# Searches in alternating pairs, and the background of an activation phase as three paced streams

## The chip, the cores and the metric

One core of a Trainium2 chip runs the whole kernel. Its engines are TensorE (PE; its weight loads are shown apart as PEld), VectorE (DVE), ScalarE (ACT), GpSimd (POOL) and SyncE (SP, which here only issues transfers). The metric is the device time of one execution in microseconds, lower is better; the figure of a kernel is the median of its runs.

## The reference

One layer of a streaming encoder over 512 tokens of width 1024. First a token mixer (a gated short convolution and a gated linear recurrence), which this change does not touch. Then a channel part that looks up experts by product keys, which is where all of this takes place. Cut to its core:

```
N_KEYS, PEER_HEADS, PEER_TOPK = 128, 8, 16          # 128*128 experts
q  = (xb @ w_q).reshape(p, PEER_HEADS, 2, 64)
sc = einsum('phcd,hcnd->phcn', q, sub_keys)          # scores of 128 sub-keys, twice per head
top_s, top_i = top_k(sc, 16)                         # stage 1: 16 of 128, for c = 0, 1
cand_s = top_s[:, :, 0, :, None] + top_s[:, :, 1, None, :]
cand_i = top_i[:, :, 0, :, None] * N_KEYS + top_i[:, :, 1, None, :]
best_s, best_pos = top_k(cand_s, 16)                 # stage 2: 16 of the sums
idx = take_along_axis(cand_i, best_pos)
g   = softmax(best_s)
act  = gelu(einsum('phkd,pd->phk', expert_u[idx], xb))
out  = einsum('phk,phkd->pd', g * act, expert_v[idx])
```

The layer ends with a gated residual add and a final RMSNorm.

## The kernel before

The 512 tokens stand in four tiles of 128 (`t` = 0 to 3). Tokens from 192 on (320 of them, `NU`) are treated densely: the activations of all 16,384 experts are computed by TensorE, 128 experts at a time, and multiplied by a gate that is zero for experts not chosen. The first 192 tokens are treated sparsely for the activation: the chosen rows of `expert_u` are gathered from HBM by GpSimd's indirect transfers, and a dot product on VectorE (`scr`) gives each activation. Tile 0 is sparse to the end: for it rows of `expert_v` are gathered and summed (`ys`). The 64 tokens of tile 1 in between (`XB`) have sparse activations and dense outputs.

All large products are made of three matmuls in a rounded format: weights are loaded as `wraw`, ACT rounds them to `whi`, DVE subtracts to get the remainder `wlo`, and each block is multiplied high by high, high by low and low by high (lines 90, 91, 92). DVE's `wlo` of a chunk is thus needed before TensorE reaches the chunk's third matmul.

The stages that matter here, in order of time:

- **Query phase** (to about 310 us): queries and sub-key scores; the 32 stage 1 searches of heads 0 to 3 are woven in by the scheduler.
- **Activation phase** (from about 310 us; `CE` = 124 of the 128 "u" chunks before the next phase begins): a chunk is 24 matmuls into `ps_act` and a gelu on ACT (`act`). Beside this runs the background work: the remaining stage 1 searches, the four `topk_tile`, the gates, and the dots.
- **Output phase** (from about 878 us): 128 "v" chunks of 18 matmuls into `acc`, together with the last four "u" chunks; the dots that are left and the 128 row sums of tile 0 run beside it.

A search (`top16`, lines 448 to 454) is five operations of VectorE: the eight largest, their places, the same values struck out, the next eight, their places. Each reads what the operation before wrote. Stage 1 searches 128 scores (`top`, `sc`), stage 2 searches 64 candidate sums (`best`, `cand`).

A gate group (`gates_step`) serves four tokens: DVE compares for one factor (`jh`, line 601) and part of the other (`igh`, line 611), ACT makes the rest of `igh` by two activations (lines 608 and 609), TensorE multiplies them (`ps_gt`, line 617), ACT copies the result to a staging tile (`stg`, line 626), and every four groups SP stores it to HBM (`Gd`); one of these stores, the last, is issued by ACT. There are 96 groups: 80 for tiles 1 (second half), 2 and 3, which need only the top-k of their tile, and 16 for the `XB` tokens, which need their 64 dots first. The output phase loads gates back (`gt`, line 858) and multiplies them with `act` (`cf`, line 880).

The order in the activation phase is fixed when the kernel is built: in that part nothing is rescheduled, and every engine runs its instructions in the order in which they were written. A planner keeps an estimate of time for PE, DVE and ACT (`pe`, `dve`, `ac`). After each chunk it takes steps from generators as long as DVE's estimate is behind PE's; each step `yield`s what it costs on DVE, or `None` for "not before the next chunk". In the kernel before there are two generators, the background `bg` and the dots `dot_gen`. The background is one long sequence: searches, top-k of tile 1, the remaining searches, top-k of tile 0, gates of tile 1 mixed with the top-k of tile 2, gates of tile 2 mixed with the top-k of tile 3, gates of tile 3, gates of the `XB` tokens. `SH` sets the share of the dots. In the loop of chunk `k`, DVE's work for the chunk after next (`wlo` of `k + 2`) is written first, and the background steps follow it.

Of the kernel before, what the change touches and what calls it, by code (L numbers as in the profile page):

```python
# [8 lines left out]
F32 = mybir.dt.float32  # L9
# [11 lines left out]
NT = 4  # L21
NE = 128
# [12 lines left out]
def block_kernel(ctx, tc, xT, small, w_ada1, w_ada, b_ada, w_in, w_r, w_i, w_out, w_q, keys, uT, u, v, final_g, out):  # L35
    nc = tc.nc
# [196 lines left out]
    z_, tn, e_, w_, w2, ac = (l4[:, i, :] for i in range(6))  # L233
# [85 lines left out]
    for cb in range(4):  # L319
# [14 lines left out]
        r = mt("r")  # L334
# [3 lines left out]
        s = mt("s")  # L338
# [4 lines left out]
        a = mt("a")  # L343
# [5 lines left out]
        h = mt("h")  # L349
# [92 lines left out]
    scp = ep.enter_context(tc.tile_pool(name="scp", bufs=1, side="right"))  # L442
# [2 lines left out]
    scx = ExitStack()  # L445
    scs = scx.enter_context(tc.tile_pool(name="scs", bufs=1, side="right"))

    def top16(best, where, s, width):
        rep = scp.tile([128, 128], F32, name="rep", bufs=2)[:, :width]
        nc.vector.max(out=best[:, 0:8], in_=s)  # L450
        nc.vector.max_index(out=where[:, 0:8], in_max=best[:, 0:8], in_values=s)
        nc.vector.match_replace(out=rep, in_to_replace=best[:, 0:8], in_values=s, imm_value=-3.0e38)
        nc.vector.max(out=best[:, 8:16], in_=rep)
        nc.vector.max_index(out=where[:, 8:16], in_max=best[:, 8:16], in_values=rep)

    sc = {}

    def stage1(heads, tiles):
        for t in tiles:
            for h in heads:  # L460
                for c in range(2):
                    top16(top[:, t, h, c], ti[:, t, h, c], sc[h, c][:, t, :], 128)
                    yield 1000

    qsp = {}
    early = chain(*(stage1([h], range(NT)) for h in range(HQ)))
# [52 lines left out]
    selT = {}  # L519
# [4 lines left out]
    def topk_tile(t):  # L524
# [11 lines left out]
        yield 1900  # L536
        best = topk.tile([128, 8, 16], F32, name="best")
        pos = topk.tile([128, 8, 16], U32, name="pos")
        for h in range(8):
            top16(best[:, h], pos[:, h], cand[:, h, :], 64)  # L540
            yield 700
        g = g_s.rearrange("p (h k) -> p h k", h=8) if t == 0 else topk.tile([128, 8, 16], F32, name="g")
        nc.vector.tensor_sub(g, best, best[:, :, 0:1].to_broadcast([128, 8, 16]))
        msk = topk.tile([128, 8, 16], U32, name="msk")
# [35 lines left out]
        else:  # L580
# [9 lines left out]
            if t == 1:  # L590
# [4 lines left out]
                for e in range(2):  # L595
                    nc.vector.tensor_copy(idx_b[XB * e:XB * (e + 1), :], idf[0:XB, XB * e:XB * (e + 1)])
        yield 1200

    def gates_prep(sl, t0, aoh):
        jh = topk.tile([128, 4, 128], F32, name="jh", bufs=3)  # L600
# [19 lines left out]
    gst = {}  # L620
# [37 lines left out]

    stgp = []

    def merge(a, b, share):
        da = db = 0.0
        live = [a, b]
        while live:
            g = a if (len(live) == 2 and da * (1 - share) <= db * share) or live == [a] else b
            if g not in live:
                g = live[0]
            n = next(g, 0)
            if n == 0:
                live.remove(g)  # L670
                continue
            if g is a:
                da += n or 1200
            else:
                db += n or 1200
            yield n
# [67 lines left out]
    def dots():  # L744
        for n, (_, hn, dst, k) in enumerate(usteps):
            for m in range(n, min(n + ahead() - 1, len(usteps))):
                assert m < XB or len(sready) == 2
                gath(u, usteps[m][0], usteps[m][3], m)
            scr = rowp.tile([128, D], F16, name="scr")
            nc.vector.scalar_tensor_tensor(scr, rows.pop(n), 1.0, hn, op0=OP.mult, op1=OP.mult,  # L750
                                           accum_out=dst[:, k:k + 1])
# [5 lines left out]
            yield 1270  # L757

    def sums():
        for k in range(128):  # L760
            for kk in range(k, min(k + ahead() - 1, 128)):
                gath(v, idx_s, kk, kk)
            if k == 0:
                nc.vector.tensor_scalar(ys, rows.pop(k), acts[:, 0:1], None, op0=OP.mult)
            else:
                nc.vector.scalar_tensor_tensor(ys, rows.pop(k), acts[:, k:k + 1], ys, op0=OP.mult, op1=OP.add)  # L766
            if k == 3:
                coef_gelu(1)
            if k == 8:
                coef_gate(1)  # L770
            yield 1270


    hd = lambda k: h2h[:, k, T - NU:]
# [108 lines left out]
            nc.scalar.activation(ch, cf, AF.Copy)  # L883
            coef[n + 2] = (cf, ch)

    bg = background_E()
    dot_gen = dots()
    pe, dve, ac = [0], [0], [0]
    td = tb = 0
    first = None  # L890
    done = False
    for k in range(5):
        w_load(k)
    for k in range(3):
# [5 lines left out]
    for k in range(CE):  # L900
        weights(k)
        u_chunk(k, psE)
        if sready and first is None:
            first = k + 4
# [3 lines left out]
        dve[0] = max(dve[0], RHO * pe[0] - LEAD)  # L908
        hold = done
        xd = 0  # L910
        while dve[0] < RHO * pe[0] or (k == CE - XE - 1 and not done):
            if done and xd >= XD:
                break
            if first is not None and k >= first and (hold or td * (1 - SH) < tb * SH or (gst and ac[0] > pe[0] + AD)):
                n = next(dot_gen, None)
                if n:
                    dve[0] += n
                    td += n
                    xd += 1
                    continue  # L920
            if hold:
                break
            n = next(bg, 0)
            if n == 0:
                done = hold = True
                kb = k
                continue
            if n is None:
                hold = k < CE - XE - 1
                continue  # L930
            dve[0] += n
            if first is not None:
                tb += n
        w_high(k + 3)
        if k == CE - XE - 1:
# [44 lines left out]
        nc.vector.tensor_add(frow[0], frow[0], frow[1])  # L980

    sparse = chain(dot_gen, sum_gen)
    steps, given = len(usteps) - len(bdone) + 128, 0
    for k in range(CE, len(jobs)):
        w_load(k + 5)
        w_high(k + 3)
        w_low(k + 2)
        kind, n = jobs[k]
        if kind == "u":
            u_chunk(k, psP)  # L990
        else:
            v_gates(n + 5)
            v_coef(n)
            vsp[n] = [w.pop(k).rearrange("p k e -> p (k e)") for w in (whi, wlo)] + list(coef.pop(n))
            if n < NE - VT:
                for b in range(3):
                    v_chunk(n, b)
                del vsp[n]
            u_evict()
            pe[0] += 4090  # L1000
            dve[0] += 2005
        if kind == "v":
            share = min((n + 1) / (NE - VE), 1) * (steps + 0.31 * (NE - RB)) - 0.31 * max(n + 1 - RB, 0)
            while given < share and next(sparse, None):
                given += 1
    fin = vp.tile([128, 2, 3, D], F32, name="gt", bufs=1)
    final_rows()
    manual.close()
# [42 lines left out]
LEAD = 3500  # L1051
RHO = 1.0
VE = 1
SH = 0.44
XD = 1
CE = 124
GB_E = 4
# [55 lines left out]
```

## Time and profile before

| what | us |
|---|---|
| median of 3 runs | 1439.85 (1435.31 to 1441.27) |
| the profiled execution's own time | 1442.91 |
| its span, first to last instruction | 1441.1 |
| TensorE busy | 1368.3 |
| VectorE busy | 1258.8 |
| ScalarE busy | 750.2 |
| GpSimd busy | 488.7 |

The profiled execution is 3.06 us above the median, and 1.8 us of its time lies outside the span. TensorE's matmuls overlap, so that a matmul whose duration is given as 0.31 us may start every 0.147 us; a short rest of the engine does not always show as idle time, and starts are the better measure. The same is true of VectorE: the next operation may start before the end shown for the one before. A row of the waits reads: engine, tile and line that waited; what ended the wait; total, number and longest wait in us. The mark q behind an engine means its queue, which issues transfers.

### The profile page before, as it was taken

To read this page: it belongs to the slowest core of one execution; us is meant where nothing else is said; L and a number is where in the kernel's file an instruction comes from. 1 tells how busy PE (TensorE), PEld (TensorE's weight loads), DVE (VectorE), ACT (ScalarE), POOL (GpSimd) and SP (SyncE) were. 2 spreads that over 40 slices of the span, in tenths; PEclk is the share of its full clock that TensorE was granted. 3 is DMA by queue.
4 is the path that set the end of the run, shared out by engine and by line. 5 is a ranking of instruction groups with operands and counts; after the bars stand their busy time and mean duration, and the time that the engine had idled before them with its cause. 6 is when DMAs were issued, how large, how long until landed. Compare 5 with 4: busy or idle time off the path is not lost.

```text
span 1441.1 us, 22491 instructions
## 1 busy us (share of the span) xinstructions
PE 1368.3 (95%) x7739; PEld 1179.2 (82%) x7739; DVE 1258.8 (87%) x2600; ACT 750.2 (52%) x1336; POOL 488.7 (34%) x334
## 2 busy tenths in 40 slices
PE   6999998999988998989999997999999999999995
PEld 2566787789988988989999997877788888888884
DVE  6776555898999999989999995889989899999998
ACT  3554433435433678889999543433434344343443
POOL 0000000000232343234344343556655565655550
PEclk9999999999999999999999998999999999999998
DMA  9575322124588989989999999999999999999994
GB/s 382 201 273 188 120 86 91 66 97 147 188 282 273 317 281 321 335 297 319 349 379 368 354 366 363 342 384 408 405 410 404 411 404 412 411 412 411 410 376 174
DMA packets 160759, 440.14 MB, mean 305 GB/s; under 512 B 16258, under 2 KB 68482, under 8 KB 158596
## 3 DMA queue, kind: packets, MB, share of 16 engines
q1 hardware_dynamic: 113636, 267.76, 50.6%
q0 software_dynamic: 46720, 169.89, 31.1%
q8 instruction: 61, 1.00, 0.3%
q10 hardware_dynamic: 288, 1.05, 0.2%
q14 instruction: 54, 0.44, 0.1%
HBM read 393.54 MB, written 45.09 MB: 304 GB/s over the span
## 4 chain that ended last, share of the span: by engine, by line
PE 44%; DVE 20%; issue 16%; DMA 13%; POOL 3%; ACT 3%; SPq 0%; DVEq 0%; ACTq 0%; POOLq 0%
PE acc L967 17%; DMA wraw<-in_v_dram 7%; PE ps_z L90 5%; PE ps_z L92 5%; PE ps_z L91 5%; DVE scr L750 4%; DVE wlo L81 4%; POOL rows L730 3%; DMA rows<-in_u_dram,idx_s 2%; PE ps_act L90 2%; PE ps_act L91 2%; PE ps_act L92 2%; DMA rows<-in_u_dram,idx_b 2%; DVE cl L873 1%; PE ps_gt L617 1%
## 5 line engine op out<-in xcount | busy, mean ns | idle before, releaser
L76 ACT ACTIVATE whi<-wraw 128x1024 fp32r<-128x1024 f32 x292 | 308.2, 1056 | 315.3 <-DMA wraw<-in_v_dram 127.6
L81 DVE TENSOR_TENSOR wlo<-wraw,whi 128x1024 fp32r<-128x1024 f32 x292 | 355.8, 1219 | 72.8 <-ACT whi L76 71.6
L92 PE MATMUL ps_act<-h,wlo 128*128 128x320 f32 x1024 | 319.3, 312 | 9.9 <-DVE wlo L81 9.7
L90 PE MATMUL ps_act<-h,whi 128*128 128x320 f32 x1024 | 323.1, 316 | 3.5 <-ACT act L816 2.3
L91 PE MATMUL ps_act<-h,whi 128*128 128x320 f32 x1024 | 317.9, 310 | 0.0
L730 POOL DMA_INDIRECT rows<-in_u_dram,idx_s x128 | 192.7, 1506 | 226.5 <-DVE scr L750 208.5
L730 POOL DMA_INDIRECT rows<-in_v_dram,idx_s x128 | 197.8, 1545 | 150.2 <-DVE ys L766 123.6
L967 PE MATMUL acc<-whi,ch 128*128 128x512 f32 x750 | 233.1, 392 | 9.2 <-ACT act L816 7.4
L967 PE MATMUL acc<-whi,cl 128*128 128x512 f32 x750 | 233.5, 393 | 0.4
L967 PE MATMUL acc<-wlo,ch 128*128 128x512 f32 x750 | 232.0, 390 | 0.0
L92 PEld LDWEIGHTS ps_act<-h,wlo 128*128 128x128 f32 x1024 | 193.5, 189 | 13.9 <-DVE wlo L81 13.9
L90 PEld LDWEIGHTS ps_act<-h,whi 128*128 128x128 f32 x1024 | 194.0, 189 | 4.4 <-ACT act L816 2.9
L91 PEld LDWEIGHTS ps_act<-h,whi 128*128 128x128 f32 x1024 | 193.8, 189 | 0.2
L730 POOL DMA_INDIRECT rows<-in_u_dram,idx_b x64 | 93.0, 1453 | 254.5 <-DVE scr L750 109.8
L967 PEld LDWEIGHTS acc<-whi,ch 128*128 128x128 f32 x750 | 141.1, 189 | 40.3 <-ACT act L816 8.2
L967 PEld LDWEIGHTS acc<-whi,cl 128*128 128x128 f32 x750 | 140.1, 188 | 34.1 <-DVE cl L873 5.7
L967 PEld LDWEIGHTS acc<-wlo,ch 128*128 128x128 f32 x750 | 141.4, 189 | 29.8
L766 DVE SCALAR_TENSOR_TENSOR ys<-rows,acts,ys 128x1024 f32<-128x1024 f32 x127 | 162.6, 1280 | 1.5
L750 DVE SCALAR_TENSOR_TENSOR scr<-rows,h2n 128x1024 f16<-128x1024 f32 x128 | 156.1, 1219 | 6.0 <-DMA rows<-in_u_dram,idx_s 4.4
L883 ACT ACTIVATE ch<-cf 128x384 fp32r<-128x384 f32 x128 | 67.3, 526 | 120.1 <-DVE cf L880 116.7
L617 PE MATMUL ps_gt<-igh,jh 128*128 128x128 f32 x768 | 99.7, 279 | 13.7 <-DVE jh L601 8.0
L816 ACT ACTIVATE act<-ps_act 128x320 f32<-128x320 f32 x128 | 55.2, 432 | 107.0 <-PE ps_act L92 106.7
(258 smaller groups left out, 1879.7 us busy)
## 6 DMA issues: line engine op xcount, KB each, us to landing
wraw<-in_uT_dram SPq DMA_DIRECT2D x128, 512.0 KB, 5.4
wraw<-in_v_dram SPq DMA_DIRECT2D x128, 512.0 KB, 9.6
Gd<-stg SPq DMA_DIRECT2D x46, 512.0 KB, 7.2
wada<-in_w_ada_dram SPq DMA_DIRECT2D x16, 1024.0 KB, 5.1
Ad<-act SPq DMA_DIRECT2D x96, 160.0 KB, 6.9
act<-Ad SPq DMA_DIRECT2D x96, 160.0 KB, 10.7
h<-Gd SPq DMA_DIRECT2D x12, 1024.0 KB, 15.3
wraw<-in_w_in_dram SPq DMA_DIRECT2D x20, 512.0 KB, 5.8
```

The source lines that it names most:

```text
L76: nc.scalar.activation(hi, raw, AF.Copy)
L81: nc.vector.tensor_sub(lo, raw, hi.bitcast(F32))
L90: nc.tensor.matmul(ps, hi[:, k, :], xh(k), start=first and k == ks[0], stop=False)
L91: nc.tensor.matmul(ps, hi[:, k, :], xl(k), start=False, stop=False)
L92: nc.tensor.matmul(ps, lo[:, k, :], xh(k), start=False, stop=last and k == ks[-1])
L617: nc.tensor.matmul(pg[:, :, k], jh[:, k, :], ig[:, k, :], start=True, stop=True)
L730: nc.gpsimd.indirect_dma_start(out=r[:, :], out_offset=None, in_=table, in_offset=bass.IndirectOffsetOnAxis(ap=idxs[:, k:k + 1], axis=0))
L750: nc.vector.scalar_tensor_tensor(scr, rows.pop(n), 1.0, hn, op0=OP.mult, op1=OP.mult, accum_out=dst[:, k:k + 1])
L766: nc.vector.scalar_tensor_tensor(ys, rows.pop(k), acts[:, k:k + 1], ys, op0=OP.mult, op1=OP.add)
L816: nc.scalar.activation(act[c], ps, AF.Gelu)
L883: nc.scalar.activation(ch, cf, AF.Copy)
L967: nc.tensor.matmul(accs[b][e], st[:, bs], mv[:, e * 512:(e + 1) * 512], start=first, stop=last)
```

## The change

1. `top16` takes two searches at once and writes each of the five operations for the one and then for the other. Its planned cost goes from 1000 ns to 2 x 1150 for a pair of stage 1, and from 700 to 2 x 850 for one of stage 2.
2. The background is cut into three generators beside the dots: `searches_E` (top-k of tiles 1, 2, 0, 3), `rest_E` (the stage 1 searches of tiles 2, 0, 3), and `gates_E` (all gates, each tile from the chunk after its top-k). The function `turn` picks one after each chunk: gates when fewer have been given than a straight line from the first possible chunk (`gopen`) to `KG` = 4 chunks before the end asks for, searches by a budget per chunk (`NS`), the remaining searches against a number of dots per chunk (`DS`), and the dots otherwise.
3. The top-k of tile 0, on which the dots of tile 0 wait, now comes third instead of second. A dot costs 1320 in the plan instead of 1270, and DVE is planned to run up to 6000 ns further ahead in the first nine chunks (`HEAD`).

The diff, cut:

```diff
-    def top16(best, where, s, width):
-        rep = scp.tile([128, 128], F32, name="rep", bufs=2)[:, :width]
-        nc.vector.max(out=best[:, 0:8], in_=s)
...
+    def top16(two, width, cost):
+        reps = [scp.tile([128, 128], F32, name="rep", bufs=2)[:, :width] for _ in two]
+        for best, where, s in two:
+            nc.vector.max(out=best[:, 0:8], in_=s)
+        for best, where, s in two:
+            nc.vector.max_index(out=where[:, 0:8], in_max=best[:, 0:8], in_values=s)
+        for rep, (best, where, s) in zip(reps, two):
+            nc.vector.match_replace(out=rep, in_to_replace=best[:, 0:8], in_values=s, imm_value=-3.0e38)
+        yield 1.2 * cost
+        for rep, (best, where, s) in zip(reps, two):
+            nc.vector.max(out=best[:, 8:16], in_=rep)
+        for rep, (best, where, s) in zip(reps, two):
+            nc.vector.max_index(out=where[:, 8:16], in_max=best[:, 8:16], in_values=rep)
+        yield 0.8 * cost
...
-        for h in range(8):
-            top16(best[:, h], pos[:, h], cand[:, h, :], 64)
-            yield 700
+        for h in range(0, 8, 2):
+            yield from top16([(best[:, j], pos[:, j], cand[:, j, :]) for j in (h, h + 1)], 64, 850)
...
-    def background_E():
+    def searches_E():
         heads = range(HQ, 8)
         yield from stage1(heads, [1])
         yield from topk_tile(1)
         sready.append(1)
-        yield from stage1(heads, [0, 2, 3])
+        while not gopen:
+            yield None
+        yield from topk_tile(2)
+        yield from topk_tile(0)
+        sready.append(0)
+        yield from topk_tile(3)
+
+    def rest_E():
+        yield from stage1(range(HQ, 8), [2, 0, 3])
         scx.close()
         stgp.append(ep.enter_context(tc.tile_pool(name="stgp", bufs=1, side="right")))
-        yield from topk_tile(0)
-        sready.append(0)
-        yield from merge(gates_tile(1, range(4, 8), selT[1]), topk_tile(2), 0.32)
-        yield from merge(gates_tile(2, range(8), selT[2]), topk_tile(3), 0.48)
-        yield from gates_tile(3, range(8), selT[3])
+        gopen.append(cur[0])
+
+    def gates_E():
+        for t in range(1, NT):
+            while gready.get(t, NE) > cur[0]:
+                yield None
+            yield from gates_tile(t, range(4 if t == 1 else 0, 8), selT[t])
         while len(bdone) < XB:
-            yield next(dot_gen)
+            yield None
...
+    def turn(k):
+        awake = [g for g in "gsrd" if g in gens and asleep[g] <= k]
+        if gopen and "g" in gens:
+            gt = 96 * (k + 1 - gopen[0]) / (KD - KG - gopen[0])
+            if "g" in awake and given["g"] < gt and ac[0] < pe[0] + AD:
+                return "g"
+            if "s" in awake and (given["g"] < gt and ac[0] < pe[0] + AD or given["s"] < NS * (k - gopen[0]) / (KD - gopen[0])):
+                return "s"
+        elif "s" in awake:
+            return "s"
+        elif "r" in awake and ("d" not in awake or given["d"] >= DS * (k - first[0])):
+            return "r"
+        for g in "dsg" if ac[0] < pe[0] + AD else "ds":
+            if g in awake:
+                return g
...
-            if first is not None and k >= first and (hold or td * (1 - SH) < tb * SH or (gst and ac[0] > pe[0] + AD)):
-                n = next(dot_gen, None)
...
-            n = next(bg, 0)
+            n = next(gens[g], 0)
```

What this does to the order of instructions is seen best at two places. The first is VectorE around the 25th of the 124 chunks, each begun by its `wlo` (line 81). Before, there stand pairs of dots (`scr`), then single searches (`top`, `ti`, `rep`), and no gates:

```order
L81 TENSOR_TENSOR wlo<-wraw,whi 128x1024
L750 SCALAR_TENSOR_TENSOR scr,act_b<-rows,h2b 128x1024 x2
L81 TENSOR_TENSOR wlo<-wraw,whi 128x1024
L450 MAX top<-sc 128x8
L451 MAX_INDEX ti<-top,sc 128x8
L452 MATCH_REPLACE rep<-top,sc 128x128
L453 MAX top<-rep 128x8
L454 MAX_INDEX ti<-top,rep 128x8
L750 SCALAR_TENSOR_TENSOR scr,act_b<-rows,h2b 128x1024
```

After, in the same place, a gate group (`jh`, `igh`) follows each `wlo`, then dots or part of a pair of narrow searches (`best`, `pos`):

```order
L81 TENSOR_TENSOR wlo<-wraw,whi 128x1024
L606 TENSOR_TENSOR jh<-iota,selT 128x512
L616 TENSOR_SCALAR igh<-iota,selT 128x128
L751 SCALAR_TENSOR_TENSOR scr,act_b<-rows,h2b 128x1024 x2
L81 TENSOR_TENSOR wlo<-wraw,whi 128x1024
L606 TENSOR_TENSOR jh<-iota,selT 128x512
L616 TENSOR_SCALAR igh<-iota,selT 128x128
L451 MAX best<-cand 128x8 x2
L453 MAX_INDEX pos<-best,cand 128x8 x2
L455 MATCH_REPLACE rep<-best,cand 128x64 x2
L751 SCALAR_TENSOR_TENSOR scr,act_b<-rows,h2b 128x1024
```

The wide searches of this stretch have moved some chunks ahead, gates have moved here from about chunk 48 on, and the operations of two searches alternate (x2).

The second place is ScalarE from the last copies of gates (`stg`) to the first gate that the output phase reads (`cf`). Before, three copies stand in one chunk, then the last store of gates, and four pairs of `whi` and `act` before the `cf`:

```order
L626 ACTIVATE stg<-ps_gt 128x128x4 x3
L637 DMA Gd_2592<-stg 128x1024 x2
L76 ACTIVATE whi<-wraw 128x1024
L816 ACTIVATE act<-ps_act 128x320
L76 ACTIVATE whi<-wraw 128x1024
L816 ACTIVATE act<-ps_act 128x320
L76 ACTIVATE whi<-wraw 128x1024
L816 ACTIVATE act<-ps_act 128x320
L76 ACTIVATE whi<-wraw 128x1024
L816 ACTIVATE act<-ps_act 128x320
L76 ACTIVATE whi<-wraw 128x1024
L879 ACTIVATE cf<-gt 128x64
```

After, the last copy comes a chunk ahead of the store, and two more pairs of `whi` and `act` (six, the first three shown) stand between the store and the `cf`:

```order
L631 ACTIVATE stg<-ps_gt 128x128x4
L76 ACTIVATE whi<-wraw 128x1024
L817 ACTIVATE act<-ps_act 128x320
L642 DMA Gd_2592<-stg 128x1024 x2
L76 ACTIVATE whi<-wraw 128x1024
L817 ACTIVATE act<-ps_act 128x320
L76 ACTIVATE whi<-wraw 128x1024
L817 ACTIVATE act<-ps_act 128x320
L76 ACTIVATE whi<-wraw 128x1024
L817 ACTIVATE act<-ps_act 128x320
```

The store has moved two chunks ahead; on TensorE the last `ps_gt` has moved from behind the chunk numbered 118 to behind 114.

Over the phase, in the order: 118 dots stand ahead of the `wlo` numbered 128, against 122 before; the gates run in chunks 22 to 36, 46 to 67 and 88 to 113 instead of 46 to 118; and around chunks 70 to 77, until the top-k of tile 0 is done, no dots can be given.

More of the change, by code (lines that the diff above doesn't have):

```diff
@@ L460, in stage1 @@
             for h in heads:
-                for c in range(2):
-                    top16(top[:, t, h, c], ti[:, t, h, c], sc[h, c][:, t, :], 128)
-                    yield 1000
+                yield from top16([(top[:, t, h, c], ti[:, t, h, c], sc[h, c][:, t, :]) for c in range(2)], 128, 1150)
     qsp = {}
@@ L597, in topk_tile @@
         yield 1200
+        gready[t] = cur[0] + 1
     def gates_prep(sl, t0, aoh):
@@ L659, in block_kernel @@
     stgp = []
[L661 to L676, printed above, removed]
     sready = []
-    def background_E():
+    cur, gready, gopen = [0], {}, []
+    def searches_E():
         heads = range(HQ, 8)
@@ L746, in dots @@
             for m in range(n, min(n + ahead() - 1, len(usteps))):
-                assert m < XB or len(sready) == 2
+                while m >= XB and len(sready) < 2:
+                    yield None
                 gath(u, usteps[m][0], usteps[m][3], m)
@@ L756, in dots @@
                 coef_gate(0)
-            yield 1270
+            yield 1320
     def sums():
@@ L884, in v_coef @@
             coef[n + 2] = (cf, ch)
[L886 to L891, printed above, removed]
+    gens = {"s": searches_E(), "r": rest_E(), "g": gates_E(), "d": dots()}
+    dot_gen = gens["d"]
+    pe, dve, ac = [0], [-HEAD], [0]
+    late_k = {}
+    asleep = {"s": 0, "r": 0, "g": 0, "d": NE}
+    given = {"s": 0, "r": 0, "g": 0, "d": 0}
+    KD = CE - XE - 1
+    first = []
+    def turn(k):
[13 more added lines that the diff above has]
+                return g
     for k in range(5):
@@ L902, in block_kernel @@
         u_chunk(k, psE)
-        if sready and first is None:
-            first = k + 4
+        cur[0] = k
+        if sready and not first:
+            first.append(k + 4)
+            asleep["d"] = k + 4
             for m in range(GB_E - 1):
@@ L907, in block_kernel @@
         ac[0] = max(ac[0], pe[0] - LEAD)
-        dve[0] = max(dve[0], RHO * pe[0] - LEAD)
-        hold = done
+        dve[0] = max(dve[0], RHO * pe[0] - LEAD - (HEAD if k < 9 else 0))
         xd = 0
-        while dve[0] < RHO * pe[0] or (k == CE - XE - 1 and not done):
-            if done and xd >= XD:
-                break
-            if first is not None and k >= first and (hold or td * (1 - SH) < tb * SH or (gst and ac[0] > pe[0] + AD)):
-                n = next(dot_gen, None)
[L916 to L922, printed above, removed]
-            n = next(bg, 0)
+        while dve[0] < RHO * pe[0] or k == KD:
+            g = turn(k)
+            if k == KD:
+                g = next((g for g in "sg" if g in gens), None)
+                if "s" not in gens and len(bdone) < XB:
+                    g = "d"
+            if g is None or (g == "d" and "g" not in gens and xd >= XD):
+                break
+            n = next(gens[g], 0)
             if n == 0:
-                done = hold = True
-                kb = k
+                assert g != "d"
+                late_k[g] = k
+                del gens[g]
                 continue
             if n is None:
-                hold = k < CE - XE - 1
+                asleep[g] = k + 1
                 continue
             dve[0] += n
-            if first is not None:
-                tb += n
+            xd += g == "d"
+            if gopen or g == "d":
+                given[g] += 1 if g in "gd" else n
         w_high(k + 3)
-        if k == CE - XE - 1:
+        if k == KD:
             ep.close()
@@ L982, in block_kernel @@
     sparse = chain(dot_gen, sum_gen)
-    steps, given = len(usteps) - len(bdone) + 128, 0
+    steps, done = len(usteps) - len(bdone) + 128, 0
     for k in range(CE, len(jobs)):
@@ L1003, in block_kernel @@
             share = min((n + 1) / (NE - VE), 1) * (steps + 0.31 * (NE - RB)) - 0.31 * max(n + 1 - RB, 0)
-            while given < share and next(sparse, None):
-                given += 1
+            while done < share and next(sparse, None):
+                done += 1
     fin = vp.tile([128, 2, 3, D], F32, name="gt", bufs=1)
@@ L1053 @@
 VE = 1
-SH = 0.44
+KG = 4
+HEAD = 6000
+NS = 60000
+DS = 1.0
 XD = 1
```

6 lines of the change are left out of this document (1 added, 5 removed).

## The prediction

> **What bounds the kernel now.** I read the page's engine shares first, then stretches of time, the matrix engine's waits, and single rows. The stretches of the activation phase (128 chunks of 24 matmuls, 124 of them before the first `acc`) come first; columns are stretch, length, busy us of PE, PEld, DVE, ACT, POOL with instruction counts, granted clock, DMA share, GB/s.
>
> ```profile
> PE 1368.3 (95%) x7739; PEld 1179.2 (82%) x7739; DVE 1258.8 (87%) x2600; ACT 750.2 (52%) x1336; POOL 488.7 (34%) x334
> 309.60:872.40 562.80, 536.04 (x3755) 528.58 (x3755) 521.37 (x1295) 381.58 (x723) 182.45 (x123) 0.99 0.85 301
> 309.60:386.00 76.40, 75.50 (x504) 75.23 (x505) 68.03 (x253) 36.42 (x51) 3.86 (x4) 0.98 0.46 157
> 386.00:471.00 85.00, 75.03 (x486) 71.04 (x485) 80.75 (x255) 33.15 (x44) 29.56 (x20) 1.00 0.78 260
> 471.00:565.00 94.00, 89.34 (x622) 87.92 (x623) 89.59 (x199) 69.95 (x129) 31.97 (x22) 1.00 0.88 307
> 565.00:700.00 135.00, 124.49 (x878) 123.11 (x877) 123.56 (x272) 117.97 (x248) 49.10 (x33) 0.97 0.92 323
> 700.00:800.00 100.00, 100.00 (x756) 100.00 (x755) 96.49 (x190) 94.95 (x208) 42.56 (x28) 1.00 1.00 367
> 872.40:886.40 14.00, 6.57 (x17) 4.67 (x15) 9.34 (x14) 5.71 (x11) 3.86 (x3) 0.63 1.02 343
> 886.40:1150.00 263.60, 261.43 (x1170) 213.80 (x1169) 239.26 (x350) 104.68 (x185) 150.30 (x101) 1.00 1.01 393
> 1150.00:1400.00 250.00, 250.00 (x1105) 207.00 (x1104) 240.20 (x281) 107.59 (x189) 144.68 (x93) 1.00 1.03 407
> ```
>
> PE never rests from 700 to 800 and after 1150, though DVE and ACT are about 95% busy there. It does rest 10.0 us in 386–471, 4.7 in 471–565, 10.5 in 565–700, and at the change of phase 17 matmuls take 14 us. Its waits in 309.6–887:
>
> ```profile
> PE ps_act L92 <- DVE wlo L81: 9.7, 12, 1.4
> PE ps_gt L617 <- DVE jh L601: 8.0, 4, 2.7
> PE acc L967 <- ACT act L816: 7.4, 2, 5.0
> PE ps_gt L617 <- ACT sqd L608: 2.6, 1, 2.6
> ```
>
> Next, PE's own price. Two L90 matmuls, 96 apart (four chunks), and two gate groups in the chain of waits:
>
> ```profile
> 315.57 0.31 PE L90 MATMUL ps_act<-h,whi 128*128 128x320 f32 x1
> 329.65 0.31 PE L90 MATMUL ps_act<-h,whi 128*128 128x320 f32 x1
> 820.50 1.78 PE ps_gt L617 x16
> ```
>
> A chunk is 14.08 / 4 = 3.52 us, a gate group 0.89. So 124 chunks and 96 groups are 436.5 + 85.4, with some 2 us of small transposes 524 us, against 562.8: 39 lost. Of those 39, the clock takes about 1.5 in the first stretch (0.02 of 76) and 3.5 in 565–700 (0.03 of 135 at most); about 30 are stalls, the rest jitter. From 872.4 to 886.4 the 17 matmuls are worth 17 x 0.226 (250 / 1105) = 3.8 us: 10 lost. In all 49 us.
>
> **Searches in pairs.** In the activation phase a search runs alone, each instruction reading what the one before wrote; in the query phase before it the scheduler already wove two searches. Starts of like instructions, alone, woven, then alone on 64 candidates:
>
> ```profile
> 320.37 0.28 DVE L450 MAX8 top<-sc 128x8 f32<-128x128 f32 x1
> 320.68 0.09 DVE L451 MATCH_VALUE_LOAD ti<-top,sc 128x8 f32 x1
> 321.94 0.28 DVE L450 MAX8 top<-sc 128x8 f32<-128x128 f32 x1
> ...
> 271.43 0.28 DVE L450 MAX8 top<-sc 128x8 f32<-128x128 f32 x1
> 271.63 0.27 DVE L453 MAX8 top<-rep 128x8 f32<-128x128 f32 x1
> 272.59 0.28 DVE L450 MAX8 top<-sc 128x8 f32<-128x128 f32 x1
> ...
> 328.37 0.21 DVE L450 MAX8 best<-cand 128x8 f32<-128x64 f32 x1
> 329.60 0.21 DVE L450 MAX8 best<-cand 128x8 f32<-128x64 f32 x1
> ```
>
> Alone 1.57 us, woven 1.16: the next start comes 0.20 behind a MAX8 instead of 0.31 when it does not need its result. The pair is that woven form, so a wide search saves 0.41. For the narrow one (1.23) no woven row exists: between saving 0 and 0.41; I take the same three dependent steps at 0.11, so 0.90. 32 wide and 32 narrow searches of the phase: 13.1 + 10.6 = 24 us less on DVE. The query phase gains nothing, being woven already.
>
> [...]
>
> **The three streams.** Prices of the other DVE work:
>
> ```profile
> 720.46 0.68 DVE L601 TENSOR_TENSOR jh<-iota,selT 128x512 f32<-128x512 f32 x1
> 721.06 0.59 DVE L611 TENSOR_SCALAR igh<-iota,selT 128x128 f32<-128x128 f32 x2
> 721.57 1.21 DVE L750 SCALAR_TENSOR_TENSOR scr<-rows,h2n 128x1024 f16<-128x1024 f32 x1
> ...
> 722.83 1.23 DVE L750 SCALAR_TENSOR_TENSOR scr<-rows,h2n 128x1024 f16<-128x1024 f32 x1
> 723.98 1.22 DVE L81 TENSOR_TENSOR wlo<-wraw,whi 128x1024 fp32r<-128x1024 f32 x1
> 725.12 0.69 DVE L601 TENSOR_TENSOR jh<-iota,selT 128x512 f32<-128x512 f32 x1
> ```
>
> Start to start: `jh` 0.60, `igh` 0.26 each, a dot 1.15 to 1.26 (1.2), `wlo` 1.14. With these, the search prices and the counts of the two orders, DVE against PE in us per stretch, numbered by the `wlo` that the work stands ahead of (small operations at 0.2 to 0.6, the 2048-wide ones at 1.25):
>
> before: 22–39 DVE 74, PE 64; 40–57 71, 68; 58–90 153, 153; 91–107 88, 90; 108–120 61, 62.
> after: 22–39 75, 77; 40–57 76, 82; 58–90 124, 131; 91–107 85, 88; 108–120 58, 59.
>
> The 10 us that DVE is over in 22–39 before are the 10.0 that PE rests in 386–471, so the sum holds. Afterwards PE is the longer one everywhere: gates, which PE does, stand where formerly only DVE worked, and the searches are cheaper. The cover is thin in 91–107 (3 us), but 700–800 shows that density, two gate groups a chunk, running without rest, with ACT at 94.95 of 100; the new order is hardly anywhere denser for ACT. The dots stop around chunks 70–77, as tile 0's top-k comes later, but nothing of this phase waits for them; otherwise they come at 1.2 a chunk as before, so POOL's gathers, each behind the dot that frees its buffer, keep their pace.
>
> What stays: the cold start 1.5, jitter 4, one wait for ACT at the first top-k 1. New: gates now begin, or double their rate, three times (in the loops of chunks 22, 46 and 88), each needing DVE a chunk further ahead; I charge each the mean `jh` wait, 8.0 / 4 = 2.0. One half-clock spell costs 1.7. Sum 14, so 39 − 14 = 25 gained. Bounds: 0 (each removed wait returns as another) and 34 (only start and jitter stay).
>
> [...] Here the clock mean of 0.97 stands in 565–700, where no single wait exceeds 2.7, so I keep the spell.
>
> **The change of phase.** Who waits there: SP's load of the first gates, behind PE's last gates and the last store; DVE then; the store itself:
>
> ```profile
> SPq L858 <- DMA Gd<-stg: 6.5, 1, 6.5
> SPq L858 <- PE ps_gt L617: 2.2, 1, 2.2
> 855.65 0.82 ACTq L637 DMA_DIRECT2D Gd<-stg  x2
> 874.30 0.49 DVE L880 TENSOR_TENSOR cf<-act,gt 128x320 f32<-128x320 f32 x1 [7.42 <-DMA gt<-Gd]
> 875.49 1.06 ACT L76 ACTIVATE whi<-wraw 128x1024 fp32r<-128x1024 f32 x1 [9.47 <-DMA wraw<-in_uT_dram]
> ```
>
> While SP stands 8.7 us, the weight loads queued behind it are late, ACT waits 9.47 for one, and the `act` that frees PSUM stands behind it. In the new order PE's last gate group comes four chunks earlier (14 us) and the store's place on ACT two chunks (7 us), no longer held by `ps_gt`. SP's stop nearly goes; what is late next is the 512 KB gate load itself, which lands close to its use. I leave 4 of the 10: 6 gained (bounds 0 to 10).
>
> **Dots left over.** By the same chunk 118 dots are done instead of 122, so four rows of 128 x 4 KB, 2.1 MB, move into the second phase. At 407 GB/s that is 5.2 us if transfers bind, 0 if they don't; in 1150–1400 PE rests nowhere at 407, in 886–1150 it loses some 4. I take 2.
>
> **Sum.** −25 − 6 + 2 = −29 against the profiled run's own 1442.91 (span 1441.1): 1413.9. That run is 3.06 over the median of 1439.85, so 1411.
>
> **Rivals.** (1) Transfers take it back: the last chunks now run at 3.52 us without gates, while dots, weights and gate loads come as before; the DMA share is 1.02 there already. Then the change of phase keeps its 10 and the dots cost 5.2: −25 + 5 = −20, 1420. (2) Dots or gates hold each other: each of the 27 single gate groups woven with narrow searches (loops 22–36 and 55–66) waits 0.4 more than charged: 11 us, 1422. Against it: DVE's sum is under PE's there. [...] (4) Slower: every one of those 27 groups makes PE wait the 2.0 us of the `jh` row, since gates, searches and dots alternate on DVE with no lead: 54 us, less the 29: 1465; it decides once more than 14 of the 27 wait so. Against it: after its waits of 565–700 PE had none for 100 us at twice the gate density.
>
> **Chances.** As worked out 0.66 (its own range 1400 to 1421); rival 1 0.13, rival 2 0.10, rival 3 0.06, rival 4 0.05. The range reaches from 1400 (stalls all but gone, 34 + 10 − 5 off) to 1431, leaving out rivals 3 and 4 and the luckiest tenth. Faster by over 0.5% (7 us, about what a measurement of this kernel tells from no change) 0.89, within 0.06, slower 0.05.
>
> **What would show it.** Paired searches at 1.16 and 0.90 us; no `wlo` wait of PE in chunks 22–40; under 12 us of PE rest between 310 and the first `acc`; that `acc` near 849; SP's wait at the gate load under 2; the second phase within 3 us of its old length. I am wrong if PE waits for `ps_gt` once per woven gate group, or if the second phase loses pace to transfers.

## The result, and the profile after

The changed kernel takes 1417.0 us (median of 4 runs, 1415.15 to 1418.33) against 1440.56 for the kernel before in the same runs; the ratio is 0.9843, 95% interval 0.9815 to 0.9871. The profiled run took 1418.33 itself (span 1416.6), 24.6 us less than the 1442.91 (span 1441.1) of the one before.

Stretches of the changed kernel, with the columns of the prediction (length, busy us and instructions of PE, PEld, DVE, ACT, POOL, clock, DMA share, GB/s): the activation phase, the change of phase, the output phase to its last `acc`, and four closer looks at the output phase:

```profile
309.40:838.40 529.00, 526.42 (x3754) 524.91 (x3755) 498.98 (x1281) 383.35 (x727) 183.97 (x119) 1.00 0.87 317
838.40:852.00 13.60, 7.30 (x19) 5.23 (x18) 9.03 (x14) 5.72 (x11) 4.19 (x3) 0.62 1.03 347
852.00:1402.60 550.60, 542.15 (x2385) 445.54 (x2384) 511.14 (x679) 223.47 (x394) 303.68 (x198) 0.99 0.99 387
963.50:984.40 20.90, 17.58 (x74) 13.07 (x73) 16.65 (x27) 6.91 (x12) 12.47 (x9) 1.00 1.04 415
984.40:1002.40 18.00, 18.00 (x72) 14.67 (x73) 17.86 (x29) 7.79 (x14) 11.12 (x7) 0.91 0.91 327
1035.10:1056.10 21.00, 18.47 (x74) 14.54 (x73) 17.53 (x28) 8.48 (x15) 10.65 (x7) 0.92 1.04 411
1056.10:1072.40 16.30, 16.30 (x74) 13.50 (x72) 16.23 (x19) 7.08 (x13) 10.47 (x7) 1.00 1.03 415
```

The output phase before, cut in the same place:

```profile
886.40:1426.30 539.90, 537.48 (x2386) 442.06 (x2385) 505.59 (x668) 222.41 (x394) 297.14 (x195) 1.00 1.00 391
```

The same cuts before are 562.8, 14.0, 539.9 (to the last `acc` at 1426.3) and then 14.8 to the end; now 529.0, 13.6, 550.6 and 14.0. So the 24.5 us of span are −33.8, −0.4, +10.7 and −0.8, and 0.2 that the phase begins earlier: the activation phase gained more than the whole change did, and the output phase gave a third of it back. PE's waits from 309.4 to 853, all of them:

```profile
PE acc L987 <- ACT act L817: 6.3, 2, 3.9
PE ps_act L90 <- ACT sc L494: 1.2, 1, 1.2
PE ps_gt L622 <- ACT stg L631: 0.9, 1, 0.9
PE ps_gt L622 <- ACT igh L614: 0.8, 2, 0.5
PE ps_act L90 <- ACT act L817: 0.4, 1, 0.4
PE ps_gt L622 <- DVE igh L616: 0.3, 1, 0.3
```

The waits for `wlo` (9.7) and `jh` (8.0) are gone; the one at the change of phase (first row) is not. The searches, each row now two instructions (the two halves of a narrow pair, and the start of the next pair):

```profile
320.61 0.35 DVE L451 MAX8 best<-cand 128x8 f32<-128x64 f32 x2
321.65 0.35 DVE L458 MAX8 best<-rep 128x8 f32<-128x64 f32 x2
322.31 0.34 DVE L451 MAX8 best<-cand 128x8 f32<-128x64 f32 x2
```

A pair starts 1.70 us behind the one before it: 0.85 a search, against 1.23 alone. At the change of phase, SP's issues of the gate loads and what stood behind them (the second row is the next weight load's issue):

```profile
823.26 7.21 SPq L859 DMA_DIRECT2D gt<-Gd  x3
830.58 3.03 SPq L71 DMA_DIRECT2D wraw<-in_uT_dram  x1
835.64 6.87 SPq L859 DMA_DIRECT2D gt<-Gd  x3
838.09 0.49 DVE L881 TENSOR_TENSOR cf<-act,gt 128x320 f32<-128x320 f32 x1 [5.27 <-DMA gt<-Gd]
840.54 1.06 ACT L76 ACTIVATE whi<-wraw 128x1024 fp32r<-128x1024 f32 x1 [8.34 <-DMA wraw<-in_uT_dram]
```

SP no longer waits for the gates' store, but the issue of three loads itself holds it for 7.21 us; the weight load behind them is 7 us late and ACT waits 8.34 for it. The same loads before, in three closer views of SP (855 to 856.2, 862.3 to 862.95, 870 to 877.55):

```profile
855.02 1.00 SPq L858 DMA_DIRECT2D gt<-Gd  x2
862.55 0.36 SPq L858 DMA_DIRECT2D gt<-Gd  x1
870.09 7.43 SPq L858 DMA_DIRECT2D gt<-Gd  x3
```

The first three were issued in 1.4 us, with the 6.5 us wait for the store between the second and the third; the next three, with no wait among them, took 7.43 already. In the output phase PE waits 2.6 and 2.5 us in two places (at 981 and 1039); what was waited for in the few us around each:

```profile
PE acc L987 <- ACT ch L884: 2.6, 1, 2.6
ACT whi L76 <- DMA wraw<-in_v_dram: 7.4, 1, 7.4
...
PE acc L987 <- ACT ch L884: 2.5, 1, 2.5
DVE cf L881 <- DMA act<-Ad: 4.0, 1, 4.0
```

And the two transfers in the chain of waits of that stretch (start, length):

```profile
964.16 18.31 DMA wraw<-in_v_dram
1020.49 17.95 DMA act<-Ad
```

A weight load took 18.31 us and an activation load 17.95, where their medians in this kernel are 10.0 and 11.0, at DMA shares of 1.03 and 1.04. Each wait is followed by about eight matmuls at half clock, 0.43 us instead of 0.227 (clocks of 0.51 from 984.9 to 988.3 and 0.50 from 1043.1 to 1046.3, which make the 0.91 and 0.92 above). So the two cost some 4.6 us each: 2.6 to 2.8 for the wait and some 1.6 for the spell, the rest in short gaps beside them. The second shows in one stretch, the sixth above: 72 matmuls take 21.0 us, 16.3 in the quiet seventh. The first wait lies in the fourth stretch and its spell in the fifth. Another 3 us are lost at the end: in the last 62.6 us to the last `acc` 261 matmuls run, against 275 before.

### The profile page after: what moved, and what is told of

Read it like the earlier page. It is cut to its first block, busy times and chain, and to the rows that moved or that the text cites. A ratio compares the mean times of both kernels' runs of the same rounds, so it can differ in the third digit from the quotient of the medians.

```text
span 1416.6 us, 22503 instructions
## 1 busy us (share of the span) xinstructions
PE 1363.8 (96%) x7739; PEld 1179.4 (83%) x7739; DVE 1241.4 (88%) x2598; ACT 753.0 (53%) x1340; POOL 497.1 (35%) x334
## 4 chain that ended last, share of the span: by engine, by line
PE 43%; issue 21%; DVE 14%; DMA 13%; POOL 6%; ACT 1%; SPq 1%; DVEq 0%; POOLq 0%; ACTq 0%
PE acc L987 18%; POOL rows L730 6%; DMA wraw<-in_v_dram 6%; PE ps_z L90 5%; PE ps_z L92 5%; PE ps_z L91 5%; DVE scr L751 3%; DMA rows<-in_u_dram,idx_s 2%; DVE wlo L81 2%; PE ps_act L90 2%; PE ps_act L92 2%; PE ps_act L91 2%; DVE cl L874 2%; DVE ys L767 1%; DMA act<-Ad 1%
## 5 line engine op out<-in xcount | busy, mean ns | idle before, releaser
L730 POOL DMA_INDIRECT rows<-in_u_dram,idx_b x64 | 99.1, 1548 | 211.7 <-DVE scr L751 109.1
L406 POOL DMA_DIRECT2D x1d<-xn x8 | 4.6, 578 | 281.8 <-DVE wlo L81 234.4
```

Source lines behind the costliest of these rows:

```text
L730: nc.gpsimd.indirect_dma_start(out=r[:, :], out_offset=None, in_=table, in_offset=bass.IndirectOffsetOnAxis(ap=idxs[:, k:k + 1], axis=0))
```

## The experiments

Times are medians; in brackets the runs' range. "E" is the time from the first `ps_act` matmul to the first `acc`, "V" from there to the last `acc`: before 568.0 and 548.7, after 533.2 and 559.9. A gap is counted from the last `ps_act` matmul's start to the first `acc`'s: 5.35 before, 4.22 after. Every ratio is to the kernel before, run beside it. E, V and gaps come from the one profiled execution of each kernel, while the runs of one kernel lie up to some 10 us apart, and the profiled one of the kernel before is 3 us over its median; so differences of under about 3 us in E or V are not told from none.

**e1_pairs.** The kernel before with the pairs alone; costs, order of streams and gates as before.

```diff
-    def top16(best, where, s, width):
+    def top16(two, width, cost):
...
-                for c in range(2):
-                    top16(top[:, t, h, c], ti[:, t, h, c], sc[h, c][:, t, :], 128)
-                    yield 1000
+                yield from top16([(top[:, t, h, c], ti[:, t, h, c], sc[h, c][:, t, :]) for c in range(2)], 128, 1000)
```

> The kernel before with the searches in alternating pairs and nothing else (planned costs per search, streams and order as before). Theory (VectorE's sum against TensorE's, stretch by stretch): the 24 us come off VectorE, but only where it was the longer engine is time gained: in the stretch of chunks 22 to 39 the 10 us rest of TensorE falls to about 3, the rests among the gates (10.5 us in 565 to 700) and at the change of phase (10 us) stay. Gain 6 to 12 us, 1429 to 1435. Rival, the pairs do nothing: 1440. Rival, the pairs do it all: 1417. The paired searches are expected at 1.16 us wide and 0.90 us narrow per search.

Measured 1414.42 (1414.27 to 1417.33), ratio 0.984 (0.9807 to 0.9872): as much as the whole change, as the rival "the pairs do it all" had it. E 539.3, V 548.7.

```profile
309.00:849.30 540.30, 526.16 (x3756) 523.91 (x3756) 505.36 (x1298) 383.37 (x729) 180.32 (x123) 1.00 0.90 317
849.30:1397.00 547.70, 542.97 (x2395) 446.56 (x2396) 512.47 (x679) 226.32 (x400) 302.12 (x197) 0.99 1.00 391
```

PE's largest wait in its activation phase (us, times, longest):

```profile
PE ps_gt L621 <- DVE jh L605: 5.2, 3, 2.2
```

My figure of 1429 to 1435 was wrong: I kept the rests among the gates. But most of them were DVE's debt from the searches. By the prediction's own prices DVE's sum in 22–39 falls from 74 to 65 against PE's 64, in 58–90 from 153 to 149 against 152, and the `wlo` waits vanish.

**e2_streams.** The changed kernel with the streams, but each search's five operations in a row again.

```diff
-        for best, where, s in two:
+        for n, (rep, (best, where, s)) in enumerate(zip(reps, two)):
...
-        yield 1.2 * cost
-        for rep, (best, where, s) in zip(reps, two):
...
+            if n == 0:
+                yield 1.2 * cost
```

> The changed kernel with its streams, order and planned costs, but the two searches of a pair written one after the other instead of alternating. Theory: VectorE has 24 us more work and is over TensorE again by about 5 us in the stretch of chunks 22 to 39; elsewhere the streams leave it room. The activation phase is 5 to 12 us longer than in the changed kernel: 1422 to 1429. Rival, order alone matters: 1417. Rival, the pairs carry the whole gain: 1440.

Measured 1436.64, ratio 0.9982 (0.9962 to 1.0001): not told from no change. E 554.8, V 555.8.

```profile
309.00:864.40 555.40, 532.82 (x3756) 526.79 (x3756) 519.11 (x1289) 386.04 (x733) 184.31 (x119) 0.99 0.85 304
```

PE's largest wait there, which the pairs had removed:

```profile
PE ps_act L92 <- DVE wlo L81: 6.7, 9, 1.7
```

So alone the streams win 13.2 in E and lose 7.1 in V, 6 us net where the medians show 3; on top of the pairs they win 6.1 and lose 11.2. My 1422 to 1429 was wrong here too; the rival that gave the pairs the whole gain (1440) came nearer.

**e3_fewer_rows.** The changed kernel without the transfers of eight row tiles (4.2 MB) in the output phase; those dots read the row before again.

```diff
+        if table is u and key in range(141, 157, 2) and key not in rows:
+            rows[key] = rows[key - 1]
```

> The changed kernel without the transfers of 8 gathered rows tiles, 4.2 MB, about chunks 12 to 20 of the output phase: the 8 dots are still made, on the rows of the dot before, so this part of the output is not the reference's. The output phase of the changed kernel is 11 us longer than before from its first accumulation on. Theory, transfers bind there: 4.2 MB at 388 GB/s are up to 10.8 us, of which at most the 7 to 9 us of stalls between 923 and 1046 us can come back: 1408 to 1411. Rival, VectorE binds there: no change, 1417.

Measured 1413.14 (1412.07 to 1415.2), ratio 0.9827 (0.9795 to 0.9859), between the 1408 to 1411 expected and the rival's 1417. V 554.5: 5.4 of the 11.2 come back, for twice the bytes of the four dots left over. A row tile (0.52 MB, 1.3 us at the 404 GB/s of 1110–1380) is so worth 0.7 us, by this one profile: transfers are a part of V's loss, not all of it.

**e7_xd2.** The changed kernel with two chunks, instead of one, kept for dots at the end of the activation phase: 124 dots ahead of the output phase in DVE's order instead of 118.

```diff
-XD = 1
+XD = 2
```

> The changed kernel with two dots instead of one allowed per chunk behind the last gates (XD = 2): 124 dots instead of 118 stand before the output phase. Theory, leftover dots are paid for in the output phase by their transfers at about 1.35 us each: 6 of them give 8 us there, less what they take from the first gate loads at the change of phase (up to 4 us): 1409 to 1414. Rival, the change of phase is itself bound by transfers and pays the same back: 1416 to 1420.

Measured 1411.49 (1410.54 to 1413.99), ratio 0.9815 (0.9782 to 0.9847). V falls by 9.1 to 550.8, E grows by 2.2: six dots moved win 1.5 us of V each, twice what leaving a tile's transfer out had won. With a moved dot its 1.2 us of DVE leave the phase as well as its bytes, which e3_fewer_rows left there; the two were not tried apart. Of the 2.2 in E, 2.1 are the gap ahead of the first `acc`, 6.28 instead of 4.22.

**e8_dot1200, e8_dot1000.** The same with dots planned at a smaller cost, so that more of them stand early: 133 and 157.

```diff
-            yield 1320
+            yield 1200
```

(1000 in the second; both with `XD = 2`.)

> The changed kernel with two chunks of the activation phase kept for dots at its end (as in e7_xd2) and a planned cost of 1200 ns for a dot, so that 133 dots of the first tile stand ahead of the output phase in VectorE's order instead of 118 (124 in e7_xd2). Theory: a dot left over costs the output phase about 1.5 us, and the activation phase has room for it (VectorE busy 500.12 of 533.20 us there in the changed kernel): activation phase 533 to 538 us, output phase 535 to 541, the time 1397 to 1404. First rival, the output phase is held by its transfers and not by the dots: it stays at 547 to 556, the time 1409 to 1417. Second rival, VectorE sets the activation phase already: the phase grows by some 1.2 us for each of the nine dots beyond e7_xd2, to 545 to 548, and the time stays at 1409 to 1414.

> As e8_dot1200, but a dot planned at 1000 ns: 157 dots stand ahead of the output phase, 39 more than in the changed kernel. Theory (room of some 33 us on VectorE in the activation phase, 1.2 us for a dot): 39 dots are 47 us, 14 more than the room, so the activation phase grows to 545 to 555 us and the output phase ends at what its matmuls allow, 533 to 540: the time 1407 to 1419, worse than with 133 dots. Rival, a dot is worth 1.5 us in the output phase without end and costs nothing before it: output phase under 515, the time under 1385. Second rival, transfers hold the output phase: 548 to 556 there, the time over 1425.

Measured 1416.87 (1415.19 to 1419.27), ratio 0.9841 (0.9813 to 0.987), and 1464.39 (1460.46 to 1465.73), ratio 1.0156 (1.0126 to 1.0187). The activation phase, then the output phase, of the first:

```profile
309.40:854.00 544.60, 526.78 (x3756) 523.57 (x3756) 516.94 (x1313) 383.44 (x726) 205.95 (x134) 0.99 0.89 322
854.00:1399.80 545.80, 539.74 (x2399) 447.03 (x2400) 502.72 (x660) 226.34 (x401) 281.36 (x186) 0.99 0.99 385
```

Of the second:

```profile
309.40:907.50 598.10, 542.77 (x3755) 535.62 (x3755) 546.58 (x1360) 387.27 (x729) 230.89 (x157) 0.97 0.88 314
907.50:1450.10 542.60, 538.89 (x2399) 447.89 (x2400) 477.74 (x612) 229.18 (x400) 204.29 (x163) 0.99 0.97 364
```

The row of doses (118, 124, 133, 157 dots) is E 533.2, 535.4, 544.5, 598.1 and V 559.9, 550.8, 545.9, 542.6. A dot is worth 1.5 us in V for the first six and 0.5 for the next nine, while in E it costs 0.4, then 1.0, then 2.2; the gap ahead of the first `acc` is a part of that (8.90 and 9.61 in these two). PE's largest wait in the activation phase of the second:

```profile
PE ps_gt L622 <- DVE jh L606: 16.9, 21, 3.3
```

My 33 us of room on DVE were not there to be filled: DVE ran its work in the order written, and dots whose rows were late, or that stood ahead of a `jh`, stopped PE long before DVE was full (546.58 of 598.10 busy at the worst, where from 300 to 860 DVE waited 16.3 us for rows and PE 16.9 for `jh`).

**e6_xe7.** The changed kernel with the first loads of the output phase begun two chunks earlier.

```diff
-XE = 5
+XE = 7
```

> The changed kernel with the first loads of the output phase (gates, activations, coefficients) begun seven chunks ahead of the change of phase instead of five; the dots stay at 118. Theory, the change of phase loses 9.9 us because the three gate loads are issued for 7.21 us and land late under busy transfers: two chunks more (8.4 us) hide most of it, the loss between the last activation matmul and the output matmuls' full pace falls to 3 to 6 us, VectorE no longer waits for gt, the time 1411 to 1414. Rival, the change is held by the weight load behind them (whi waits for uT by 8.3 us) or by the gelu of the last chunk's sum: the loss stays at 8 to 11, the time 1415 to 1419.

Measured 1418.34 (1417.35 to 1419.08), ratio 0.9844 (0.9817 to 0.9871): no change, though the gap ahead of the first `acc` falls from 4.22 us to 0.15 and DVE no longer waits for `gt`. SP's issue, and ACT behind it:

```profile
818.33 7.61 SPq L859 DMA_DIRECT2D gt<-Gd  x3
835.05 1.06 ACT L76 ACTIVATE whi<-wraw 128x1024 fp32r<-128x1024 f32 x1 [8.40 <-DMA wraw<-in_uT_dram]
```

The late weight load went two chunks forward with the gate loads, and PE stops 3.58 us at 832.91 instead, for the `act` behind that `whi`. So it is not the gates' landing.

**e4_gates_pool.** The changed kernel with the six gate loads at the change of phase issued by GpSimd.

```diff
-                nc.sync.dma_start(gt[:, 8 * t - 8:8 * t], Gd[t][:, :, cc:cc + 8, :].rearrange("g j i t -> j g i t"))
+                nc.gpsimd.dma_start(gt[:, 8 * t - 8:8 * t], Gd[t][:, :, cc:cc + 8, :].rearrange("g j i t -> j g i t"))
```

> The changed kernel with the output phase's first two times three gate loads issued by GpSimd, ahead of the gathers that stand there, instead of by SyncE. Theory of the issue, SyncE standing 7.21 us and 6.87 us at these loads holds up the weight loads behind them: with them elsewhere the uT load is out some 7 us earlier, ScalarE no longer waits 8.3 us for it, the change of phase loses 5 to 7 us instead of 9.9, the time 1411 to 1414. Rival of the landing, the transfers themselves are full, and the gates land when they can, whoever issues them: VectorE still waits 3 to 8 us for gt, the time 1416 to 1420.

Measured 1410.05 (1406.74 to 1413.17), ratio 0.979 (0.9757 to 0.9823). E 528.9, V 554.5.

```profile
818.97 2.79 POOL L859 DMA_DIRECT2D gt<-Gd  x3
822.43 0.33 SPq L71 DMA_DIRECT2D wraw<-in_uT_dram  x1
834.82 1.06 ACT L76 ACTIVATE whi<-wraw 128x1024 fp32r<-128x1024 f32 x1 [2.33 <-DMA wraw<-in_uT_dram]
```

The same three loads take 2.79 us of POOL instead of 7.21 of SP, the weight load goes out in time, the gap is 0.15 us. So the issue on SP was the cause of the gap, which is worth the 4.3 us of E and 1.9 of V's 5.4 (the first eight `acc` starts take 4.4 us instead of 6.3); the landing rival said 1416 to 1420. The other 3.5 us of V were in neither theory: with the same 118 dots PE's two stops are all but gone, its longest wait from 950 to 1060 being 1.3 us.

**e10_pool_xd2, e12_pool_xd2_xe7.** Both helpful edits at once (`nc.gpsimd` and `XD = 2`); then the same with the loads two chunks earlier (`XE = 7`).

> The two changes that helped, together: the output phase's first gate loads issued by GpSimd (e4_gates_pool) and two chunks kept for dots at the end of the activation phase (e7_xd2, 124 dots ahead instead of 118). Theory, two separate causes that add: the change of phase shows a gap near 0.2 us and the activation phase stays at 529 to 532 us, the output phase falls from 554.5 to 546 to 551 us by six dots at about 1 to 1.5 us; the time 1401 to 1407. Rival, both act on the same waits of the output phase: its length stays at 552 to 556 and the time at 1408 to 1413.

> As e10_pool_xd2, with the first loads of the output phase begun two chunks earlier (seven instead of five ahead), so that the two times three gate loads stand behind 50 and 54 gathers in GpSimd's queue instead of 52 and 56 (50 and 52 in e4_gates_pool). e10_pool_xd2 lost 10.4 us at the change of phase: a dot waited 7.64 us for its row, and the coefficients stood behind it on VectorE. Theory, the gate loads there went out 7 us later than in e4_gates_pool and met the last rows under full transfers: earlier, the gap falls to 0.2 to 3 us, no dot there waits over 3 us, the output phase stays near 551 us; the time 1403 to 1410. Rival, two chunks with extra dots next to the change are what makes the rows late, whenever the gates are loaded: a dot still waits 5 us or more, the gap stays at 6 to 11, the time 1414 to 1421.

Measured 1419.93 (1418.83 to 1422.04), ratio 0.9851 (0.9828 to 0.9874), and 1425.12 (1422.24 to 1426.26), ratio 0.988 (0.9842 to 0.9917). They don't add; neither of my theories for the first had this. E is 539.9 and V 552.8 in the first: what is lost lies in E. DVE and ACT of the first at the change of phase:

```profile
841.82 1.23 DVE L751 SCALAR_TENSOR_TENSOR scr<-rows,h2n 128x1024 f16<-128x1024 f32 x1 [7.64 <-DMA rows<-in_u_dram,idx_s]
848.64 0.48 DVE L881 TENSOR_TENSOR cf<-act,gt 128x320 f32<-128x320 f32 x1
849.22 0.52 ACT L884 ACTIVATE ch<-cf 128x384 fp32r<-128x384 f32 x1 [9.22 <-DVE cf L881]
```

The same of the second, and what it moved from 815 to 850:

```profile
837.92 1.23 DVE L751 SCALAR_TENSOR_TENSOR scr<-rows,h2n 128x1024 f16<-128x1024 f32 x1 [7.91 <-DMA rows<-in_u_dram,idx_s]
856.78 0.52 ACT L884 ACTIVATE ch<-cf 128x384 fp32r<-128x384 f32 x1 [15.60 <-DVE cf L881]
```

```profile
DMA packets 4568, 14.14 MB, mean 404 GB/s; under 512 B 505, under 2 KB 1405, under 8 KB 4565
```

A dot waits for its row, `cf` stands behind the dot in DVE's order, `ch` and then the `act` that PE needs stand behind `cf`: gaps of 10.38 and 6.81 us ahead of the first `acc`. Loading the gates earlier did not help, as the second run's rival had it, though the test is not clean: counted as the doses above, the second kernel has 126 dots ahead, the first 124. The 14.14 MB went at 404 GB/s, the pace of 1110–1380 in the changed kernel. But dots next to the change are not enough to make a row late: in e7_xd2, with the same 124 dots and the gates on SP, no dot waits over 2.2 us for its row, at 396 GB/s from 810 to 846. What e10_pool_xd2 adds to it is that the gates share GpSimd's queue with the rows, and in e4_gates_pool the two gathers issued right behind the gate loads there (828 to 832) landed after 16.5 and 16.6 us, against a median of 8.0. This points at the queue; another queue for the gates beside these dots was not tried.

**e11_pairs_pool.** The kernel before with the pairs and the gate loads on GpSimd, without the streams (the edits of e1_pairs and e4_gates_pool).

> The kernel before with the searches in alternating pairs (as e1_pairs) and the first gate loads of the output phase on GpSimd, without the paced streams. Theory, the loads' issue on SyncE costs the change of phase whatever the order of the searches: e1_pairs's gap of 4.63 us goes to near 0.2, the activation phase falls from 539.3 to 533 to 536, the output phase by 0 to 4 from 548.7; the time 1405 to 1411, as fast as the changed kernel with the same edit. Rival, the streams are what makes this edit pay, since e1_pairs's GpSimd queue is behind with its gathers there: the time 1412 to 1418.

Measured 1410.12 (1407.59 to 1412.81), ratio 0.9783 (0.9751 to 0.9814): the same as e4_gates_pool, E 535.4 and V 548.1 instead of 528.9 and 554.5. The streams win 6.5 in one phase and lose 6.4 in the other. These two have the lowest medians, some 7 us under the changed kernel; the intervals of their ratios and of its ratio (0.9815 to 0.9871) overlap by under 0.001. e7_xd2 (1411.49) is not told from them.

## Why the prediction was right, and where it was not

1411 was forecast and 1417.0 measured, with the right sign and inside the range. But three of its terms were mis-sized, two of them past their own bounds or nearly so, by 9 us one way and 6 and 9 the other, and they cancel in part: that the sum came out within 6 us is partly luck.

- **PE's price** holds: 524 us of PE work, now done in 529.0.
- **The pairs** hold, 0.85 us for a narrow search (0.90 forecast) and 1.18 for a wide one in e1_pairs (start to start; 1.16 forecast). Rival 3, in which they save nothing, did not occur: in e1_pairs only the order of the same operations changed, and the time fell to 1414.42. The change without the pairs' 24 us, 1411 + 24 = 1435, is what e2_streams measured (1436.6), so the 24 were the right price of the pairs.
- **The residue of 14 us** in the activation phase was the first mis-sized term: 5 stay, so 33.8 were gained instead of 25, at the edge of the bound of 34. I charged three starts of the gates the mean `jh` wait of before, 2.0 each, and a half-clock spell of 1.7 (before, the clock was 0.57 from 572 to 576, behind a wait of 2.6, and again from 623 to 627: 4 us x (1 − 0.57) = 1.7 lost each time). Those waits had come from DVE being behind; with DVE ahead all waits at `ps_gt` together are 2.0, and the mean clock of the phase is 1.00. The mean of a wait taken where an engine is late is no price for the same place when it no longer is.
- **The change of phase** was the second: 6 forecast, 0.4 measured. The step that failed is "SP's stop nearly goes". SP's 8.7 us of waits did go, but the three loads, which before took 1.4 us to issue around the 6.5 us wait, now took 7.21: of the 10.1 us that SP stood there before, 7.2 stayed. The price stood in the profile before: three such loads without a wait took 7.43. Why their issue on SP takes so long, no run shows. "What is late next is the gate load itself" was wrong too: it is the weight load behind it (e6_xe7 against e4_gates_pool).
- **Dots left over** were the third: +2 forecast, bounds 0 to 5.2, measured +10.7. The upper bound took the four tiles' bytes at the phase's pace; by e3_fewer_rows' 0.7 us a tile they are worth about 3. What it left out is that single late loads can stop PE: two that landed some 7 to 8 us over the median did so, for 2.6 and 2.5 us, and behind each stop some eight matmuls ran at half clock. That is 9 us of the loss. A late load need not cost that much: before, a weight load issued at 938.5 took 19.5 us, and PE's only wait there was 1.1. e7_xd2 gives back 9.1 with six dots, but e4_gates_pool all but loses the stops with none moved. So that the four dots alone make the loss is not shown, and why just those two loads are late and stop PE is not settled.
- **The streams** were credited with the rests among the gates. e1_pairs shows that the pairs remove most of those by themselves; the streams add 6 us there and lose 6 to 11 in the output phase. So the pairs alone give as much as the whole change, and the prediction's account of the streams as a part of the gain did not hold.
- **The signs promised**: the pairs' prices, no `wlo` wait and PE's rests held; SP's wait at the gate load is gone as well, but its issue took 7.21 us in place of it. The first `acc` came at 842.7 instead of 849, and the output phase grew by 11.2 instead of at most 3; so of the prediction's two signs of being wrong the second, a loss of pace to transfers, came in part: by e3_fewer_rows about 3 us. Rivals 2 and 4 did not occur; rival 1 did in its direction, twice as large in the output phase and hidden by the larger gain ahead of it.

## What to carry to other kernels

Weave short dependent chains on VectorE before planning anything around them: two searches in turn took 0.85 us each instead of 1.23, and that alone made waits vanish that looked like a matter of order (PE's 9.7 us for `wlo`). At a queue, add the time an instruction takes to issue to the time it waits, and ask whether a wait that goes had only covered it (here 7.21 us of issue where 6.5 of wait had been); look at what is queued behind. Work moved out of a phase bound by one engine into a phase whose transfers run at a DMA share of about 1.0 can cost there more than its bytes (a dot 1.5 us, its row tile 0.7), and work moved back next to the boundary can stand ahead of what the boundary waits for (the gap of 10.38 us in e10_pool_xd2): price both ends, and run the halves of a change apart.

## What the runs showed of the hardware that I had not expected

The same three loads took 7.21 us to issue on SP and 2.79 on POOL, with transfers at 394 GB/s (823 to 831) and 409 (815 to 840); on SP before, 1.4 with a pause of 6.5 among them and 7.43 without. Two gathers right behind the gate loads on POOL landed after 16.5 and 16.6 us, against a median of 8.0; the eight issued there from 815 to 840 had one of 13.0. After waits of PE of 2.5 and 2.6 us in the changed kernel (2.84 and 3.00 from one matmul's start to the next) some eight matmuls ran at half clock, 0.43 us instead of 0.227. Eight of them are 8 x 0.43 = 3.4 us. What brings such a spell on and what ends it, no run here shows.
